# A softmax kernel whose fourth and later loads wait until the first has landed

## The chip, the cores and the metric

The kernel runs on one core of a Trainium2 chip. The metric is the device time in microseconds (us). "Landed" means that the completion semaphore of a transfer has reached its full count (16 increments for each of the 23 transfers in the trace before).

## The reference

```python
# x: float32 of shape (16, 1024, 512)
x_max = np.max(x, axis=-1, keepdims=True)
exp_x = np.exp(x - x_max)
return (exp_x / np.sum(exp_x, axis=-1, keepdims=True)).astype(np.float32)
```

This is 33.6 MB in and 33.6 MB out, with little arithmetic per byte.

## The kernel before

The 16,384 rows go through in ten chunks of 3, 5, 8 and seven times 16 rows per partition. All loads are issued on the sync engine's queue (SP), the stores on ScalarE's. Of each chunk VectorE takes the row maxima, ScalarE the exponentials with their sums, and VectorE the reciprocals and the scaling in place. In the trace the 23 transfers land on eight semaphores, two or three on each, and the built program has a wait where one is used again.

```python
CHUNKS = [
    (3, 0), (5, 3), (8, 8), (16, 16), (16, 32), (16, 48), (16, 64), (16, 80), (16, 0), (16, 16),
]                                  # rows per partition, place in the SBUF buffer
EARLY = 8                          # loads issued at the start
AT_HEAD = {mybir.EngineType.SP: 1} # so many loads go ahead of the start barrier
# ...
    def load(k):
        queue = nc.scalar if k in ON_ACT else nc.sync
        queue.dma_start(out=place[k], in_=src[k])
# ...
    with tc.manual_schedule():
        for k in range(EARLY):
            load(k)
        # ... row maxima, exponentials, scaling and stores, group by group
```

In the built program load 0 stands ahead of the start barrier, loads 1 to 4 directly behind it. Load 5 waits for load 0 and load 6 for load 1, because they share semaphores (load 0 landed at 4.46 us and load 5 went out at 4.47 us; load 1 landed at 7.50 us and load 6 went out at 7.51 us).

Of the kernel before, what the change touches and what calls it, by code (L numbers as in the profile page):

```python
# [1 line left out]

# [4 lines left out]

F32 = mybir.dt.float32
EXP = mybir.ActivationFunctionType.Exp
AX = mybir.AxisListType.X  # L10


CHUNKS = [
    (3, 0), (5, 3), (8, 8), (16, 16), (16, 32), (16, 48), (16, 64), (16, 80), (16, 0), (16, 16),
]
SBUF_ROWS = 96

EARLY = 8
AFTER_STORE = {2: [8], 3: [9]}

GROUP = 8

FINISH_BEFORE = (1, 2, 3)

STORE_ROWS = {3: 8, 4: 8, 5: 8}

ON_ACT = ()

AT_HEAD = {mybir.EngineType.SP: 1}



def loads_at_the_head(nc):

    main, body = nc.main_func.blocks[0], nc.main_func.blocks[1]
    for engine, count in AT_HEAD.items():
        loads = [
            i
            for i in body.instructions
            if i.engine == engine and type(i).__name__ == "InstDMACopy"  # L40
        ][:count]
        barrier = next(
            n
            for n, i in enumerate(main.instructions)
            if i.engine == engine and type(i).__name__ == "InstDrain"
        )
        for load in loads:
            body.instructions.remove(load)
        main.instructions[barrier:barrier] = loads


@with_exitstack
def kernel(
    ctx: ExitStack,
    tc: tile.TileContext,
    x: bass.AP,
    out: bass.AP,
):
    nc = tc.nc
    nc.at_finalize(loads_at_the_head)  # L60
    P = nc.NUM_PARTITIONS

    x_flat = x.flatten_outer_dims()
    out_flat = out.flatten_outer_dims()
    n, d = x_flat.shape
    assert n == P * sum(R for R, _ in CHUNKS)


    src, dst, at = [], [], 0
    for R, _ in CHUNKS:  # L70
        for flat, views in ((x_flat, src), (out_flat, dst)):
            part = flat[at : at + P * R, :]
            views.append(part.rearrange("(p r) d -> p r d", r=R))
        at += P * R

    data = ctx.enter_context(tc.tile_pool(name="data", bufs=1))
    stats = ctx.enter_context(tc.tile_pool(name="stats", bufs=4))
    held = data.tile([P, SBUF_ROWS, d], F32, name="held")
    place = [held[:, s : s + R, :] for R, s in CHUNKS]


    groups = []
    for k, (R, _) in enumerate(CHUNKS):
        m = max(1, round(R / GROUP))
        cuts = [R * i // m for i in range(m + 1)]
        since = 0
        for a, b in zip(cuts, cuts[1:]):
            ends = b == R or b - since >= STORE_ROWS.get(k, R)
            groups.append((k, a, b, since if ends else None))
            since = b if ends else since  # L90
    shift = [None] * len(groups)
    sums = [None] * len(groups)

    def load(k):
        queue = nc.scalar if k in ON_ACT else nc.sync
        queue.dma_start(out=place[k], in_=src[k])

    def rowmax(g):
        k, a, b, _ = groups[g]
        shift[g] = stats.tile([P, b - a], F32, name="shift", tag="shift")  # L100
        nc.vector.reduce_max(  # L101
            out=shift[g], in_=place[k][:, a:b, :], axis=AX, negate=True
        )

    def exps(g):
        k, a, b, _ = groups[g]
        sums[g] = stats.tile([P, b - a], F32, name="sums", tag="sums")
        for r in range(a, b):
            nc.scalar.activation(  # L109
                out=place[k][:, r, :],  # L110
                in_=place[k][:, r, :],
                func=EXP,
                bias=shift[g][:, r - a : r - a + 1],
                scale=1.0,
                accum_out=sums[g][:, r - a : r - a + 1],
            )

    def scale(g):
        k, a, b, since = groups[g]
        recip = stats.tile([P, b - a], F32, name="recip", tag="recip")  # L120
        nc.vector.reciprocal(out=recip, in_=sums[g])  # L121
        for r in range(a, b):
            nc.vector.tensor_scalar_mul(  # L123
                out=place[k][:, r, :],
                in0=place[k][:, r, :],
                scalar1=recip[:, r - a : r - a + 1],
            )
        if since is not None:
            nc.scalar.dma_start(
                out=dst[k][:, since:b, :], in_=place[k][:, since:b, :]  # L130
            )
        if b == CHUNKS[k][0]:
            for later in AFTER_STORE.get(k, ()):
                load(later)
# [4 lines that stand above are left out]
        waiting = None  # L139
        for g, (k, a, _, _) in enumerate(groups):  # L140
            if waiting is not None and a == 0 and k in FINISH_BEFORE:
                scale(waiting)
                waiting = None
            rowmax(g)
            exps(g)
            if waiting is not None:
                scale(waiting)
            waiting = g
        scale(waiting)


# [1 line left out]
_INS = ['x']  # L153
_OUTS = [((16, 1024, 512), 'float32')]


# [23 lines left out]
```

## Time and profile before

| | before |
|---|---|
| time, median of the first 3 runs | 161.54 us (161.52 to 162.06) |
| span of the profiled execution | 159.7 us |
| VectorE, ScalarE busy | 78%, 58% |
| moved by DMA | 67.13 MB, mean 420 GB/s |
| load 0 issued, first packet, landed | 0.00, 1.02, 4.46 us |
| last store issued, last packet's end | 144.77, 158.53 us |

Read the DMA rows first: the transfers fill the span while no compute engine does. The lines stand in the prediction below. One more view is needed. It is not on the page: the records of single DMA packets, each with a start, a duration and a size. They don't name the DMA engine. But behind the data of each of the 23 transfers stand 16 four-byte packets (368 in all, as many as there are increments of the completion semaphores). I take one of them to be from each of the 16 engines, so that their 16 times say when each engine was done.

### The profile page before, as it was taken

The page shows a single profiled execution, that of the slowest core. Times are in us where ns is not written, and L with a number is a line of the kernel's source. Part 1 is how long each engine was busy: PE and PEld are TensorE (multiplying, and loading weights), DVE is VectorE, ACT ScalarE, POOL GpSimd, SP SyncE. Part 2 cuts the span into 40 slices and gives each one's busy share as a digit, 9 for nine tenths or more (in the row PEclk, how much of TensorE's full clock was granted, in tenths as well). Part 3 has the DMA queues.
Part 4 walks back from the last instruction along what each step waited for, and adds up shares of the span by engine and source line. Part 5 has one row for each costly group of instructions (what it writes and reads, how often), then busy time and mean ns, then how long its engine had stood idle before and what let it go on. Part 6 is the DMA issues. An engine that isn't in the chain of part 4 may idle for free.

```text
span 159.7 us, 521 instructions
## 1 busy us (share of the span) xinstructions
DVE 123.9 (78%) x162; ACT 93.3 (58%) x257; POOL 0.2 (0%) x4
## 2 busy tenths in 40 slices
DVE  0481870799699999999999999999999999762000
ACT  0718129208994959595868677686859595930000
POOL 0000000000000000000000000000000000000000
DMA  7999999899999999999999999999999999999993
GB/s 269 433 464 411 389 447 446 383 412 466 402 441 431 460 435 396 439 418 468 427 414 439 414 484 427 396 447 402 435 439 476 418 402 468 443 402 468 427 410 164
DMA packets 3315, 67.13 MB, mean 420 GB/s; under 512 B 368, under 2 KB 368, under 8 KB 624
## 3 DMA queue, kind: packets, MB, share of 16 engines
q1 hardware_dynamic: 1440, 33.56, 49.5%
q10 hardware_dynamic: 1872, 33.56, 48.9%
q14 instruction: 3, 0.02, 0.0%
HBM read 33.55 MB, written 33.55 MB: 420 GB/s over the span
## 4 chain that ended last, share of the span: by engine, by line
DVE 70%; ACT 14%; issue 3%; DMA 3%; DVEq 0%; ACTq 0%
DVE shift L101 38%; DVE held L123 30%; ACT held L109 14%; DMA held<-in_x_dram 3%; DVE recip L121 2%; DVEq L175 0%; ACTq L109 0%
## 5 line engine op out<-in xcount | busy, mean ns | idle before, releaser
L109 ACT ACTIVATE held<-held,shift 128x512 f32<-128x512 f32 x128 | 90.5, 709 | 43.4 <-DVE shift L101 33.2
L101 DVE TENSOR_REDUCE shift<-held 128x8 f32<-128x4096 f32 (+2 forms) x17 | 70.6, 4161 | 4.5 <-DMA held<-in_x_dram 4.5
L123 DVE TENSOR_SCALAR held<-held,recip 128x512 f32<-128x512 f32 x128 | 52.2, 481 | 0.6
L109 ACT ACTIVATION_READ_ACCUMULATOR held<-held,shift 128x1 f32 x128 | 24.0, 187 | 0.0
L121 DVE RECIPROCAL recip<-sums 128x8 f32<-128x8 f32 (+2 forms) x17 | 3.3, 193 | 15.8 <-ACT held L109 15.8
L109 ACT ACT_TABLE_LOAD x1 | 1.3, 1283 | 4.5 <-DMA held<-in_x_dram 4.5
L164 POOL MEMSET const-bfloat16-1.0<- 128x1 bf16 x1 | 0.1, 102 | 0.0
L164 POOL MEMSET const-uint8-127<- 128x1 uint8 x1 | 0.1, 102 | 0.0
L164 POOL MEMSET const-float32-1.0<- 128x1 f32 x1 | 0.1, 99 | 0.0
L164 POOL MEMSET const-float32-0.0<- 128x1 f32 x1 | 0.1, 98 | 0.2 <-issue 0.2
## 6 DMA issues: line engine op xcount, KB each, us to landing
held<-in_x_dram SPq DMA_DIRECT2D x7, 4096.0 KB, 41.8
out_dram<-held ACTq DMA_DIRECT2D x4, 4096.0 KB, 21.0
out_dram<-held ACTq DMA_DIRECT2D x7, 2048.0 KB, 35.5
held<-in_x_dram SPq DMA_DIRECT2D x1, 2048.0 KB, 11.3
held<-in_x_dram SPq DMA_DIRECT2D x1, 1280.0 KB, 6.7
out_dram<-held ACTq DMA_DIRECT2D x1, 1280.0 KB, 20.0
held<-in_x_dram SPq DMA_DIRECT2D x1, 768.0 KB, 4.5
out_dram<-held ACTq DMA_DIRECT2D x1, 768.0 KB, 15.7
```

The source lines that it names most:

```text
L101: nc.vector.reduce_max(out=shift[g], in_=place[k][:, a:b, :], axis=AX, negate=True)
L109: nc.scalar.activation(out=place[k][:, r, :], in_=place[k][:, r, :], func=EXP, bias=shift[g][:, r - a : r - a + 1], scale=1.0, accum_out=s ...
L121: nc.vector.reciprocal(out=recip, in_=sums[g])
L123: nc.vector.tensor_scalar_mul(out=place[k][:, r, :], in0=place[k][:, r, :], scalar1=recip[:, r - a : r - a + 1],)
L164: nc = _bacc.Bacc("TRN2", target_bir_lowering=False, num_devices=1)
```

## The change

The intent, in the words of the code: "the first load gets the descriptor generator first". Loads 3 and later are issued only once load 0 has landed. (The generator is the code's word: the traces show issues, with start and duration, and nothing of a generator.)

```diff
+ONCE_LANDED = 3
...
+    queued = [None] * len(CHUNKS)
...
     def load(k):
         queue = nc.scalar if k in ON_ACT else nc.sync
-        queue.dma_start(out=place[k], in_=src[k])
+        queued[k] = queue.dma_start(out=place[k], in_=src[k])
+        if k >= ONCE_LANDED:
+            tc.add_manual_dep(
+                queued[k].ins,
+                queued[0].ins.name,
+                mybir.DependencyInfo(
+                    mybir.DependencyClass.Sync, mybir.DependencyReason.DATA
+                ),
+                reason="the first load gets the descriptor generator first",
+            )
```

## The prediction

The sum is 161.54 us, the median of the first 3 runs, less a third of 0.7 us, so 161.3 us. That the rate stays is the author's estimate, from a DMA share of 1.00 to 1.01 at 433 GB/s between 80 and 155 us. "Generating" stands for what the author supposed to go on during an issue. The trace shows the issues alone: load 3's from 1.63 to 2.22 us, load 4's from 2.27 to 2.88 us, and none from then until 4.47 us; the first rival's slow packets of 576 to 626 ns begin in that gap, at 3.90 to 4.05 us. In this trace load 3's first packet begins at 11.25 us, after load 0's last at 4.10 us.

> **What bounds the kernel now.** I read the page first (busy shares, slices, chain, DMA queues), then the windows by stage, then the queue's issues one at a time in the timeline, and last the trace's records of single DMA packets.
>
> ```profile
> span 159.7 us, 521 instructions
> DVE 123.9 (78%) x162; ACT 93.3 (58%) x257; POOL 0.2 (0%) x4
> DMA  7999999899999999999999999999999999999993
> GB/s 269 433 464 411 389 447 446 383 412 466 402 441 431 460 435 396 439 418 468 427 414 439 414 484 427 396 447 402 435 439 476 418 402 468 443 402 468 427 410 164
> q1 hardware_dynamic: 1440, 33.56, 49.5%
> q10 hardware_dynamic: 1872, 33.56, 48.9%
> ```
>
> No engine is busy throughout: VectorE (DVE) 78%, ScalarE (ACT) 58%. The DMA digits are 9 in 37 of 40 slices, and loads (q1) and stores (q10) together fill 49.5 + 48.9 = 98.4% of the 16 DMA engines' time. So the transfers are the bound. The page's chain of waits names VectorE for 70% of the span, but that chain stops at the last instruction, which ends at about 145 us; what follows is only the DMA engines draining stores. The stages show it (us, VectorE, ScalarE, POOL, clock, DMA share, GB/s):
>
> ```profile
> 1.00:2.00 1.00, 0.00 (x0) 0.00 (x0) 0.00 (x0) 1.00 0.98 289
> 2.00:3.00 1.00, 0.00 (x0) 0.00 (x0) 0.00 (x0) 1.00 0.94 362
> 3.00:4.00 1.00, 0.00 (x0) 0.00 (x0) 0.00 (x0) 1.00 1.07 432
> 80.00:120.00 40.00, 39.82 (x52) 28.75 (x81) 0.00 (x0) 1.00 1.01 433
> 120.00:155.00 35.00, 22.12 (x38) 17.25 (x48) 0.00 (x0) 1.00 1.00 433
> 157.00:158.00 1.00, 0.00 (x0) 0.00 (x0) 0.00 (x0) 1.00 0.31 131
> ```
>
> From 3 us to 155 us the rate stays at about 433 GB/s with the engines full. Bytes over rate: 67.13 MB / 433 GB/s = 155.0 us. The packet records give the frame: first data packet at 1.02 us, last packet's end at 158.53 us. So 157.5 us between them, only 2.5 us above full rate. **Everything that the start or the end can still give lies in those 2.5 us**, plus the 1.02 us ahead of the first packet. Two of its parts are in the table: from 1 to 3 us the rate is 289 and 362 instead of 433 (lost: (144 + 71) / 433 = 0.50 us), and the end is ragged (131 GB/s from 157 to 158 us).
>
> **Where the raggedness comes from.** The packet records contain 16 four-byte packets for each transfer, one per DMA engine, behind its last data. For the first load they come at 3.11 to 3.40 us on 12 engines, and at 3.66, 3.73, 4.09 and 4.10 us on four. For the last store they come at 157.33 to 157.84 us on 12 engines, and at 158.27 to 158.52 us on four. The spread is 1.0 us at the first load and 1.2 us at the end, and much the same in between (1.15 us for the sixth load). Each engine has its own equal share of the bytes (8 packets of a 128-packet transfer) and never runs dry, so a microsecond lost in the first 4 us is still missing at the end. The late engines had slow packets: a packet of the first load takes 234 ns in the median, but 779, 599, 561 and 448 ns for some that begin between 1.88 and 2.45 us.
>
> **What is issued in that time.** The timeline of the sync queue, one issue after the other (start, duration):
>
> ```profile
> 0.00 0.37 SPq L96 DMA_DIRECT2D held<-in_x_dram  x1
> 0.78 0.33 SPq L96 DMA_DIRECT2D held<-in_x_dram  x1
> 1.16 0.42 SPq L96 DMA_DIRECT2D held<-in_x_dram  x1
> 1.63 0.59 SPq L96 DMA_DIRECT2D held<-in_x_dram  x1
> 2.27 0.61 SPq L96 DMA_DIRECT2D held<-in_x_dram  x1
> 4.47 0.33 SPq L96 DMA_DIRECT2D held<-in_x_dram  x1
> 7.51 0.33 SPq L96 DMA_DIRECT2D held<-in_x_dram  x1
> ```
>
> These are loads 0 to 6. Load 0 lands at 4.46 us and load 5 goes out at 4.47 us: it already waits for load 0, because both use the same semaphore (the instruction listing shows this wait). Loads 3 and 4 go out at 1.63 and 2.27 us and occupy the issuer for 0.59 and 0.61 us instead of 0.33 us[...].
>
> [...]
>
> **The change part by part.** The instruction listing of both kernels differs in one thing: the wait for load 0's semaphore stands before load 3 instead of before load 5. Loads 4 and 5 follow load 3 in the queue, so they come after it too. No instruction, byte, buffer or order is changed.
> - *Loads 3 and 4 go later*: from 1.63 and 2.27 us to just after load 0 lands. Three issues then follow each other: at about 4.5, 4.9 and 5.2 us if each takes 0.33 us plus the 0.05 us seen between issues, up to 5.8 us at 0.6 us each. Load 6 waits for load 1 (7.5 us) as before.
> - *Does a DMA engine run dry?* Loads 0 to 2 hold 768 + 1280 + 2048 KB = 4.19 MB, which at 433 GB/s last 9.7 us, to about 11 us. The trace has load 2's last data packet ending at 12.1 us and its earliest engine done at 11.24 us. Load 3's first packets should come about 1.0 us after its issue (load 0: issued at 0.00, first packet at 1.02 us), so at 5.5 to 6 us. This leaves 5 us to spare. Cost: 0.
> - *Load 0 is disturbed less*: if the slow packets between 1.88 and 2.9 us are due to the generating of loads 3 and 4, the two latest engines end load 0 at some 3.4 to 3.7 us instead of 4.1 us. Load 0 then lands 0.4 to 0.7 us sooner, and the whole opening moves with it.
> - *What of it reaches the end*: the opening of VectorE and ScalarE has slack against the stores and ends nothing[...]. What counts is the late engines' lag. The end is the latest engine: at most 158.52 - 157.84 = 0.7 us if all four late engines join the others. [...] the slow packets at 1.0 us (733 and 713 ns) come before load 3 is issued and stay. I credit a third: 0.7 / 3 = 0.23 us. Sum: 161.54 - 0.23 = 161.3 us.
>
> **The rivals.**
> - *Nothing at the end at all*: the lag comes from the start of HBM reading, or moves from load 0 to load 1. For it: slow packets also exist between 3.9 and 4.6 us (576 to 626 ns instead of 385 ns)[...]. Against it: nothing I can show. Time: 161.5 us.
> - *The full gain*: all four late engines join the rest and the 0.50 us lost from 1 to 3 us returns in part. For it: 12 of 16 engines already manage load 0 by 3.40 us. Time: 160.8 us.
> - *A new hole*: the new wait starves an engine. Against it: the 5 us to spare. Only if load 3 took over 5 us from issue to data would it cost anything; no issue of the trace hints at that. Time: 162 us and above.
> - *VectorE becomes the bound*: it would have to end over 3 us later than now, since its last store is issued at 144.77 us and needs only 4.19 MB / 433 GB/s = 9.7 us, while it lands at 158.86 us, 14.1 us later. An opening some tenths earlier cannot do this.
>
> **Range and chances.** Middle 161.3 us. The runs of the kernel before spread from 161.52 to 162.06 us, so the run noise is about as large as the effect. Full gain and noise below give 160.8 us, no gain with noise above gives 161.9 us. A change of 2% would need 3.2 us: more than all that is lost at the start and the end together (2.5 us), so faster by 2% is almost excluded, and slower would need a hole that nothing shows. Chances: 1% faster, 98% within 2%, 1% slower.
>
> **What would show it right or wrong.** In the timeline of the sync queue load 3 is issued within 0.05 us of load 0's landing, with 4 and 5 right behind. Load 0 lands before 4.46 us (I expect 3.8 to 4.1 us); if it doesn't, loads 3 and 4 were not what slowed it. The DMA digits stay at 9 from the second slice on; a lower digit in slices 2 to 4 would be the hole. The packets' last round shows whether the spread of 1.2 us shrank: the time should follow the latest engine. A time below 160.5 us would mean a better rate in the long middle[...]; one above 162.5 us would mean a hole or a stall that I overlooked.

## The result, and the profile after

The changed kernel took 161.72 us (median of 6 runs, 161.57 to 162.57), the kernel before 161.56 us (6 runs, 161.52 to 162.06). The ratio is 1.0013 with a 95% interval of 0.9989 to 1.0037: the same. (A ratio is the mean time of one kernel's fast runs over that of the other's fast runs of the same rounds, so it is not quite the ratio of the medians quoted here.)

The page after has the same digits and the same queue shares; span and busy times:

```profile
span 159.8 us, 521 instructions
DVE 123.9 (78%) x162; ACT 93.3 (58%) x257; POOL 0.2 (0%) x4
```

The sync queue's issues after, from the timeline in windows (start, us, then what; an x2 line merges two issues that follow each other, so the three lines overlap and show loads 3, 4 and 5):

```profile
4.51 0.33 SPq L99 DMA_DIRECT2D held<-in_x_dram  x1
4.51 0.80 SPq L99 DMA_DIRECT2D held<-in_x_dram  x2
4.88 0.91 SPq L99 DMA_DIRECT2D held<-in_x_dram  x2
```

The issues moved as meant: load 3 from 1.63 to 4.51 us, load 4 from 2.27 to 4.88 us, load 5 from 4.47 to 5.35 us. The stages of the start and the end after (us, VectorE, ScalarE, POOL, clock, DMA share, GB/s):

```profile
1.00:2.00 1.00, 0.00 (x0) 0.00 (x0) 0.00 (x0) 1.00 0.85 227
2.00:3.00 1.00, 0.00 (x0) 0.00 (x0) 0.00 (x0) 1.00 1.03 418
3.00:4.00 1.00, 0.00 (x0) 0.00 (x0) 0.00 (x0) 1.00 1.01 422
...
157.00:158.00 1.00, 0.00 (x0) 0.00 (x0) 0.00 (x0) 1.00 0.31 131
```

The second microsecond lost some rate (289 to 227 GB/s), the third won some (362 to 418); the two together moved 651 KB before and 645 KB after, so nothing was won. There is no hole. The end is as ragged as before. The packet records put the two kernels side by side; the first three rows give each engine's last record of a transfer:

```
                                    before          after
load 0, first to last engine        3.11 to 4.10    3.21 to 4.13 us
   of these, the two latest         4.09, 4.10      4.10, 4.13
last store, first to last engine    157.33 to 158.52  157.32 to 158.62
load 0 landed                       4.46            4.49
```

So load 0 lands no sooner with loads 3 and 4 out of its way, and two engines are late by about as much as before.

The records also show in what way the two are late. They can be linked engine by engine, as the ends and starts follow closely: in the kernel before 13.8 records are open on average from 1.30 to 1.85 us, and 16.0, one for each engine, from 2.05 to 3.10 us. In the kernel before, 14 engines begin load 0 by 1.26 us and the two latest only at 1.88 and 1.90 us; in the changed kernel 14 begin by 1.27 us and the two latest at 2.00 and 2.02 us. From there the two move their eight packets in 2.1 to 2.2 us, no slower than the others (the engine that began first in the changed kernel, at 1.00 us, took 2.4 us). So they start late; they are not slowed on the way.

### The profile page after: what moved, and what is told of

The parts are those of the page before. It is cut to its first block, busy times and chain, and to the rows that moved or that the text cites. A ratio compares the mean times of both kernels' runs of the same rounds, so it can differ in the third digit from the quotient of the medians.

```text
span 159.8 us, 521 instructions
## 1 busy us (share of the span) xinstructions
DVE 123.9 (78%) x162; ACT 93.3 (58%) x257; POOL 0.2 (0%) x4
## 4 chain that ended last, share of the span: by engine, by line
DVE 70%; ACT 14%; issue 3%; DMA 3%; DVEq 0%; ACTq 0%
DVE shift L113 38%; DVE held L135 30%; ACT held L121 14%; DMA held<-in_x_dram 3%; DVE recip L133 2%; DVEq L187 0%; ACTq L121 0%
```

## The experiments

Two theories from here. **Theory A:** the end is set by the latest DMA engine. Its lag arises because two of the 16 engines begin load 0 late, whatever is issued behind it. (No run took the late start away, so what it costs at the end was never measured by itself.) **Theory B** (the change's own reason): issues behind load 0 slow it. In this table "last packet" is the end of the last store packet in the profiled execution.

| run | what | median us | ratio to before [95%] | load 0's last packet | last packet |
|---|---|---|---|---|---|
| e0_after | the change again | 161.72 | 0.9975 [0.9941, 1.0010] | 4.03 | 158.49 |
| e11_after_again | the change, a third time | 162.17 | 1.0004 [0.9957, 1.0051] | 4.01 | 158.90 |
| e1_all_wait | loads 1 and 2 wait too | 164.41 | 1.0135 [1.0094, 1.0176] | 4.11 | 161.44 |
| e2_wait_load2 | loads 3 and 4 wait for load 2 | 164.48 | 1.0136 [1.0071, 1.0201] | 4.05 | 162.55 |
| e3_head5 | loads 0 to 4 ahead of the barrier | 161.55 | 0.9969 [0.9930, 1.0008] | 4.08 | 158.88 |
| e10_head5_again | the same again | 161.62 | 0.9961 [0.9923, 1.0000] | 4.06 | 158.59 |
| e4_head0 | load 0 behind the barrier | 162.28 | 1.0005 [0.9961, 1.0049] | 4.78 | 159.29 |
| e7_warm_sp | tiny load first, same queue | 161.94 | 1.0011 [0.9986, 1.0035] | 4.67 | 159.20 |
| e8_warm_act | tiny load, ScalarE's queue | 162.60 | 1.0034 [0.9992, 1.0077] | 4.01 | 159.48 |
| e9_markers | marker loads behind load 0 | 163.03 (one run) | none | 4.07 | 159.93 |
| e5_on_act | loads 3 and 4 on ScalarE's queue | 171.90 (one run) | none | 4.09 | 168.89 |

All results were correct. The kernel before, rerun beside each set, was less steady than at first: medians of 162.17, 161.65 and 162.27 us, single runs from 161.49 to 163.31 us.

### The change again

No edit: the changed kernel itself.

> The changed kernel again, for a finer interval and a second profile. Theory A (the end is set by the latest DMA engine, whose lag is that its first packet of load 0 starts about 0.9 us after the others', whatever is issued later): ratio 1.000, between 0.998 and 1.003; load 0 lands at 4.3 to 4.6 us; two engines begin load 0 at 1.8 us or later in this profile too. Theory B (loads 3 and 4 slow load 0, the change frees it): load 0 lands at 4.1 us or before, ratio 0.998 or below.

Load 0 landed at 4.38 us and two engines were late again, at 4.01 and 4.02 us against 3.27 us for the first; these two began load 0 at 1.76 and 1.80 us (1.8 us or later was expected). The second repeat, on another set:

> The changed kernel a third time, on the same chip as the run with five loads ahead of the barrier. Theory A (the change reaches nothing that sets the end): 0.998 to 1.002, load 0 at 4.3 to 4.6 us, and the measured time is the latest engine's last packet plus 3.0 us, as in all profiles so far. Theory B: 0.998 or below with load 0 at 4.1 us or before.

Load 0 landed at 4.36 us there. Over three sets the ratios are 1.0013, 0.9975 and 1.0004, and each interval contains 1. Theory B's signs (landed by 4.1 us, ratio 0.998 or below) fail on the landing in every set. The ratio of 0.9975 alone would have passed for a gain of a quarter of a per cent; it didn't come again.

### Load 0 entirely alone

```diff
-ONCE_LANDED = 3
+ONCE_LANDED = 1
```

> Loads 1 and 2 wait for load 0 as well[...]. Theory A: load 0 still lands at 4.3 us or later, with two late engines. Theory B extended (loads 1 and 2 disturb it, which the change left in place): load 0 lands at 3.9 us or before, all 16 engines within 0.4 us. Either way the engines are empty from about 4.1 to 5.5 us, and if a loss at the start is carried to the end at full size the time is 162.9 us (+1.4 us), 163.8 us if the late start of two engines comes again after the hole.

Load 0 landed at 4.45 us, with its two latest engines at 4.02 and 4.11 us. Nothing was issued behind it until 4.47 us, and still 14 engines began it by 1.26 us and these two at 2.02 and 2.17 us. This is the clearest case against theory B. The windows of this run show the hole that the waiting cost (same columns as above):

```profile
3.00:4.00 1.00, 0.00 (x0) 0.00 (x0) 0.00 (x0) 1.00 0.30 123
4.00:5.00 1.00, 0.53 (x1) 0.48 (x1) 0.00 (x0) 1.00 0.00 0
5.00:6.00 1.00, 1.00 (x1) 0.81 (x1) 0.00 (x0) 1.00 0.74 154
6.00:7.00 1.00, 0.23 (x1) 0.74 (x3) 0.00 (x0) 1.00 0.72 276
```

The DMA share falls to zero from 4 to 5 us, and the rate is still low for two microseconds after. The time was 164.4 us, more than either number (162.9 and 163.8). Load 1's last packet ends at 9.62 us instead of 7.16, which is 2.46 us later. Of this, 1.35 us is idle (4.11 us to load 1's first packet at 5.46 us). The rest is a slow restart: the first packet of an engine took 411 to 1153 ns instead of 385 ns, so load 1 needed 4.16 us instead of the 8 x 0.385 = 3.08 us of an undisturbed engine, 1.08 us more. The last packet came 2.91 us later, the time 2.89 us (164.41 against 161.52 us of the profiled runs). So in this run, where all engines lost time together, what was lost at the start is carried to the end at full size, and the restart cost nearly as much as the idle time. About 0.45 us was lost later; I did not trace it. After the hole the 16 engines end load 1 between 9.00 and 9.62 us, with no pair far behind: the late start of two engines did not come again.

### Where a wait starts to cost

```diff
-                queued[0].ins.name,
+                queued[2].ins.name,
```

> Loads 3 and 4 wait for load 2 (lands at 12.45 us) instead of load 0 (4.46 us), so their data comes at 13.5 us while the engines run out of loads at 11.2 to 12.1 us. Store 0 (0.79 MB, 1.8 us of all engines, issued at 10.0 us, first packet now at 13.9 us) can fill most of this hole, so both theories expect 161.5 to 162.3 us, with store 0 moving at about 11.5 us. A time at 161.6 us or below says that even a wait 8 us later is free.

This missed: 163.16, 163.47, 165.49 and 165.54 us. The profile is of the slowest of the four. Its windows:

```profile
11.00:12.00 1.00, 1.00 (x1) 0.00 (x0) 0.00 (x0) 1.00 0.77 303
12.00:13.00 1.00, 0.69 (x1) 0.28 (x1) 0.00 (x0) 1.00 1.00 401
13.00:14.00 1.00, 0.00 (x0) 1.00 (x3) 0.00 (x0) 1.00 0.43 180
14.00:15.00 1.00, 0.00 (x0) 1.00 (x5) 0.00 (x0) 1.00 0.09 37
15.00:16.00 1.00, 0.00 (x0) 1.00 (x3) 0.00 (x0) 1.00 1.21 344
```

Store 0 did move forward, as expected (first packet at 11.46 instead of 13.88 us), and it filled the time to about 13 us. But here the wait ended only with the slowest of 16 engines: two engines ended load 2 at 14.40 and 14.48 us, the other 14 at 12.29 us or before, and load 3 was issued at 14.79 us. So most engines stood idle until load 3's first packet at 15.74 us. Those two had already been 1.3 us behind the next latest in load 1 (8.52 and 8.53 us against 7.22 us). Why, this run doesn't tell. Together with the changed kernel this bounds the free range: the wait for load 0 costs nothing that shows, the wait for load 2 costs 1.4% (interval 0.7% to 2.0%).

### More issues beside load 0, not fewer

```diff
-AT_HEAD = {mybir.EngineType.SP: 1}
+AT_HEAD = {mybir.EngineType.SP: 5}
```

> The kernel before with loads 1 to 4 issued right behind load 0, ahead of the start barrier: the reverse of the change[...]. Theory A: load 0 lands at 4.3 to 4.6 us, time within 0.3 us of 161.55. Theory B: load 0 lands at 4.8 us or later and the time is 161.9 us or more.

Loads 1 to 4 are now issued at 0.42, 0.89, 1.36 and 2.35 us, load 3's issue lasting 0.95 us. Load 0 landed at 4.41 us. The stages of this run (same columns):

```profile
1.00:2.00 1.00, 0.00 (x0) 0.00 (x0) 0.00 (x0) 1.00 0.72 215
2.00:3.00 1.00, 0.00 (x0) 0.00 (x0) 0.00 (x0) 1.00 0.96 399
3.00:4.00 1.00, 0.00 (x0) 0.00 (x0) 0.00 (x0) 1.00 1.08 449
```

With issues going on up to 2.8 us the rate from 2 to 3 us is 399 GB/s, as much as with load 0 entirely alone (also 399), against 362 in the kernel before and 418 in the changed kernel. So issuing loads 3 and 4 in the third microsecond need not slow it; why the kernel before had 362 GB/s there, its one profile doesn't tell. The ratio looked like a small gain:

> Loads 0 to 4 all issued ahead of the start barrier, again, because its first run stood at ratio 0.9969 with an interval that just held 1. If issuing early keeps the two late engines from losing more between loads 0 and 1 (which made the slow runs of other variants), it is 0.995 to 0.998 again and few runs are above 161.9 us; if that was chance, 0.999 to 1.003.

It came out at 0.9961, with the interval ending at 1.0000; load 0 landed at 4.42 us. All 12 runs of this version lie between 161.49 and 162.36 us, while the kernel before ran from 161.50 to 163.31 us in the same two sets. The fastest runs are equal. If there is a gain, it is that slow executions are rarer: above 161.9 us lie 1 of these 12 runs, but 13 of the 22 of the kernel before in the same two sets. That is the first of the two outcomes for the repeat. But both intervals still reach 1, so I don't call it shown.

### Load 0 behind the barrier

```diff
-AT_HEAD = {mybir.EngineType.SP: 1}
+AT_HEAD = {}
```

> Load 0 issued behind the start barrier, with the others, so that all transfers start 0.4 to 0.8 us later in the trace. A lag at the start is carried to the end at full size: time 161.9 to 162.3 us (ratio 1.003 to 1.005). If the late start of two engines were tied to the moment of the program's start and not to the first large transfer, all engines would end load 0 within 0.5 us of each other and the time would stay at 161.5 to 161.8 us.

Load 0 went out at 0.73 us, its first packet came at 1.72 us, and its engines ended between 3.93 and 4.77 us. The two latest began it at 2.56 and 2.57 us, some 0.7 us later than in the kernel before: the late start moved with the load. The last packet came 0.76 us later than in the kernel before, the time of the profiled runs 162.28 against 161.52 us, also 0.76 us. The ratio of 1.0005 doesn't show it, because the kernel before ran at 161.55 to 163.31 us in that set. By profile the later start is carried over; by timing this run is inconclusive.

### A first packet to wake the engines

```diff
     with tc.manual_schedule():
+        warm = data.tile([16, 1], F32, name="warm")
+        nc.sync.dma_start(out=warm, in_=x_flat[0:16, 0:1])
         for k in range(EARLY):
```

with two loads ahead of the barrier, or, for the second run, the tiny load on ScalarE's queue.

> The kernel before with one tiny load (16 partitions x 4 bytes[...]) issued ahead of load 0 on the sync queue. Load 0 is issued some 0.37 us later. Theory A1 (two engines begin about 0.9 us late because their first use is slow to start; a first packet of any size takes that on itself): load 0's last engine begins within 0.4 us of its first, load 0 lands at 4.0 to 4.3 us, the last store's spread falls from 1.2 to about 0.7 us and the time to 161.2 us (ratio 0.998). Theory A2 (the late start belongs to the first large transfer, or to the clock time): two engines still end load 0 about 0.7 us behind the others, and all is 0.37 us later, 161.9 us (ratio 1.002).

> The same tiny load, issued from ScalarE's queue at the same time as load 0 instead of ahead of it. A1: if its packets reach the engines first, as in the run with the tiny load on the sync queue, but load 0 is delayed by at most 0.37 us; time 161.2 to 161.5 us. A2: as before, 161.5 to 161.9 us.

The 16 tiny packets of the first run all moved between 0.98 and 1.17 us. That each went through another of the 16 engines is the author's reading; the records don't name the engine. Still two engines began load 0 only at 2.30 and 2.31 us (its first packet came at 1.46 us) and ended it at 4.57 and 4.67 us, the others at 4.24 us or before. So the tiny packets didn't cure it (A1 fails): in this run the late start came with the first large transfer (A2). The ratio of 1.0011 can't tell the 0.42 us by which load 0 was issued later from nothing. In the second run load 0 was as before (4.32 us landed), but one engine ended load 1 at 8.68 us, 1.5 us behind the next latest (7.20 us), and the last packet came at 159.48 us from one engine alone, the next at 158.51 us. A2 was right on load 0; the tiny loads were no help in these two runs (ratios 1.0011 and 1.0034).

### Which engines are late

```diff
+        mark = data.tile([16, 1900], F32, name="mark")
+        load(0)
+        for n, a, c in ((4, 0, 320), (8, 320, 384), (12, 704, 448), (14, 1152, 512)):
+            nc.sync.dma_start(out=mark[0:n, a:a + c], in_=x_flat[0:n, 0:c])
-        for k in range(EARLY):
+        for k in range(1, EARLY):
```

> Which DMA engines are late: behind load 0 four small loads of 4, 8, 12 and 14 partitions with 1280, 1536, 1792 and 2048 bytes each[...]. In the packet records each engine's chain then tells by the marker packets behind its load 0 to which group it belongs. Theory A: two engines end load 0 at 4.0 us or later again, and both stand in the same group[...]; under a random cause they stand in different groups. The time is not of interest (load 3 waits for load 0 here too): 161.5 to 163 us.

There are 4, 8, 12 and 14 marker packets, and 38 more packets under 512 bytes than in the kernel before (406 against 368). So the four markers had 38 = 4 + 8 + 12 + 14 completion packets behind them, and not 16 each. With one from each engine that tells how many engines a marker went to, but not which ones. I joined the records to chains, one per engine: in these records one begins within some 8 ns of the end of the one before while the engine is busy. Sorted by the markers found behind load 0:

```
engine's load 0 done at (us)       markers behind it
3.06 to 3.65 (12 engines)          a 1792-byte one: took part in the marker of 12
3.32                               only a 2048-byte one: in the marker of 14 alone
3.71, 4.06, 4.07                   no 1792-byte one: not in the marker of 12
```

So the three latest engines are all among the four of the 16 that the marker of 12 left out, and do not look like a random choice. Which of the three carried a 2048-byte marker the records don't settle: the late ones, at 4.15 and 4.17 us, come after pauses, and one of them belongs to one of the 12. Why the late engines are among those four was not shown; this is a reading of one run, not a proof.

### Loads 3 and 4 in turn with the first ones

```diff
-ON_ACT = ()
+ON_ACT = (3, 4)
```

> The kernel before with loads 3 and 4 issued from ScalarE's queue at the start[...]. Both theories: load 0 lands at 9 to 13 us instead of 4.46 us, loads 1 and 2 after 20 us, VectorE's opening is some 8 us or more late, its slack against the stores (about 3 us) is gone and the time is 165 to 172 us. If the time stays within 1 us of 161.6, VectorE has more slack than I worked out.

The time was in the range, the reasoning half wrong. Load 0 landed at 4.43 us, not at 9 to 13: although loads 3 and 4 were issued from 0.79 us on the other queue, their first packet came at 3.79 us, when most engines had finished load 0. Loads 1 and 2 did suffer (landed at 17.4 and 32.0 us, against 7.50 and 12.45 us in the kernel before). Their landing in the issue rows of this run (KB each, us from issue to landing):

```profile
held<-in_x_dram SPq DMA_DIRECT2D x1, 2048.0 KB, 30.8
held<-in_x_dram SPq DMA_DIRECT2D x1, 1280.0 KB, 16.6
held<-in_x_dram SPq DMA_DIRECT2D x1, 768.0 KB, 4.4
```

VectorE then became the bound: from 40 to 150 us it was busy for 105.79 of 110 us, and the DMA share fell to 0.95. This run's DMA digits, in 40 slices of 4.25 us, have holes at the end where the kernel before has nines:

```profile
DMA  8999999999998999999999999999999970892885
```

The last store is issued at 158.13 us instead of 144.77 us, 13.36 us later, and the time grew by 10.38 us. The difference, 3.0 us, is the slack that VectorE had.

### What all thirteen profiles say together

Measured time minus the end of the last packet is 2.94 to 3.10 us in all thirteen profiles, from 161.48 to 171.90 us. So the time follows the latest DMA engine, plus about 3 us. Load 0's first packet came 0.99 to 1.09 us after its issue, and load 1's, issued alone in e1_all_wait, 0.99 us after (4.47 to 5.46 us). In every profile in which load 0 went out at 0.00 us the engines end it in the same pattern: the third latest at 3.60 to 3.75 us, the two latest between 3.96 and 4.13 us, whatever was issued behind; the latest was 0.75 to 1.07 us behind the first. Two of the variants that ran slow in their profile, at 162.42 us (e8_warm_act) and 163.03 us (e9_markers), show a second loss, on load 1 (last packet at 8.68 and 9.28 us instead of 7.16 us; in e9_markers load 1 was also issued later, at 2.24 us instead of 0.78 us). In these profiles a lag of one engine or a few was not carried to the end in full: measured against the kernel before, the 1.52 and 2.12 us at load 1 are 0.95 and 1.40 us at the last packet, and in e0_after load 1 ended 0.33 us later but the last packet 0.04 us sooner. (The records don't say whether the engine that ends last is the one that was late in load 1.) Whether the slow runs of the kernel before have the same cause is open, since only its 161.52 us run was profiled.

## Why the prediction was right or wrong

The time is 161.72 us, inside the range, 0.4 us above the middle, and within 2% as forecast. The range reached from the full gain to no gain with noise, so the number would have fit whether or not the change did anything; that it fits is luck as far as the mechanism of the middle goes.

- **The bound** held: the thirteen profiles tie the time to the latest DMA engine. VectorE's slack ("it would have to end over 3 us later than now") measured 3.0 us.
- **Only the wait moves** held: loads 3, 4 and 5 went out at 4.51, 4.88 and 5.35 us (expected about 4.5, 4.9 and 5.2).
- **No engine runs dry** held: the first engine ends load 2 at 11.26 us and load 3's first packet begins at 11.27 us (11.24 and 11.25 us before), and the DMA digits are the same as before.
- **"Load 0 is disturbed less"** is the step that failed. It said that the two latest engines would end at 3.4 to 3.7 us and load 0 land 0.4 to 0.7 us sooner. They ended at 4.10 and 4.13 us, and load 0 landed 0.03 us later. I had put slow packets down to the issues that went on at the same time. But the two of 599 and 561 ns, which begin at 1.88 and 1.90 us, are the first packets of the two latest engines, and first packets of other engines took up to 733 ns; these two engines were late because they began some 0.6 us after all others. Load 0 alone has the same two late engines, and five issues ahead of the barrier have them too.
- **"I credit a third"** (0.23 us at the end) falls with it: the last packet came at 158.62 instead of 158.53 us. The rival "nothing at the end at all" was right in its effect, and in placing the lag at the start of reading. What it named besides, that "the lag [...] moves from load 0 to load 1", was not seen in the changed kernel's first profile: load 1's last packet ended at 7.19 us against 7.16 us.
- **"A microsecond lost in the first 4 us is still missing at the end"** held where all engines were late together: 2.46 us lost by load 1's end gave 2.91 us at the last packet in the run with load 0 alone, and a start later by 0.70 us (first packet 1.72 against 1.02 us) gave 0.76 us. It held only in part where one or two engines were late: 1.52 and 2.12 us at load 1 left 0.95 and 1.40 us. So the 0.7 us that the prediction allowed at most for the late engines may have been too much as well; no run tested it.

What stays open is why two of 16 engines begin the first large transfer late, what the end would gain without it, and why sometimes an engine loses another 1.3 us or more in load 1.

## What to carry to other kernels

When transfers are the bound, ask which DMA engine ends last and where it lost its time; a slow packet beside an issue is no proof that the issue slowed it, and giving the suspect the machine to itself is the test. In these runs a wait that held transfers back was free while every engine still had earlier work queued (load 3 issued at 4.51 us, the first engine done with load 2 at 11.26 us: ratio 1.0013), and it ended with the slowest of the 16 engines (14.48 us in e2_wait_load2, load 3 issued at 14.79 us); so count its slack to the landing on that one, and add the restart (1.08 us in e1_all_wait). In a kernel with runs that differ by 1% a single ratio of 0.9975 is no gain: repeat it before explaining it.
